# RWKV stage of a transformer block: TensorE keeps the emitted order, PSUM banks per stream, final norms as a stream in the next unit

## The chip, the cores and the metric

One core of a Trainium2 chip runs the whole program. TensorE (PE in the profile) multiplies, VectorE (DVE), ScalarE (ACT) and GpSimd (POOL) work on tiles in SBUF and read matmul results out of PSUM, and SyncE (SP) issues most of the DMAs. Each engine takes its own instructions in a fixed order; an instruction that waits for another engine holds up everything behind it on its own. The metric is the device time of one execution in microseconds, the median of the runs.

## The reference, cut to what matters

One layer: a modulated norm, one input projection, three groups of sequence mixers that all read that projection, an output projection, a mixture of experts and a final norm. The stage that the change touches is the RWKV-7 mixer, 12 heads of 64 channels over 256 context and 512 latent tokens, once forward and once backward:

```python
def _rwkv_scan(inp, s0):
    """RWKV-7: S = S diag(w) + (S (-kk)) (kk*a)^T + v k^T ; y = S r."""
    r, decay, k, v, kk, a = (jnp.moveaxis(t, 1, 0) for t in inp)
    def step(s, t):
        rt, wt, kt, vt, kkt, at = t
        sa = jnp.einsum('bhvk,bhk->bhv', s, -kkt)
        s = (s * wt[:, :, None, :] + sa[..., None] * (kkt * at)[:, :, None, :]
             + vt[..., None] * kt[:, :, None, :])
        return s, jnp.einsum('bhvk,bhk->bhv', s, rt)
    s_fin, ys = lax.scan(step, s0, (r, decay, k, v, kk, a))
    return jnp.moveaxis(ys, 0, 1), s_fin
...
    # _rwkv_mixer, after both directions are summed
    return (_head_norm(yl, g_norm, RWKV_GN_EPS, True) + bl) * jax.nn.sigmoid(gl)
```

## The kernel before, in words

The scan is computed in blocks of 64 tokens. Within a block the step-by-step recurrence becomes small matrices, among them the inverse of a lower triangular 64x64 matrix per head, direction and block. The work is cut into 18 **units** (3 groups of four heads, 6 token blocks each), numbered 0 to 17 here. A unit passes through three stages, each a Python generator, in three consecutive steps of `rwkv_all`:

- `rw_s1`, preparation: **c**, running sums of the decays by four matmuls per half (L702); the exponentials on ScalarE; the scaled keys **BK** and queries **AR** on VectorE and GpSimd (L712 to L716); **A**, products of the two, 32 matmuls for direction 0 and then 32 for direction 1 (L729); VectorE masks them out of PSUM into **AMa** and **AMr** (L734). Then SP issues eight DMAs that write the 16x16 diagonal blocks of AMa to DRAM (**s_ad**, L741) and one that reads them back in another layout (**Lay**, L742). **T** are transposes of BK (L750). I write A\* for the last A group of a unit.
- `rw_s2`, the inverse: on VectorE a **chain** of 15 rounds (product L776 into ptm, sum L778 into Tm) inverts the 16x16 blocks from Lay; two DMAs (**s_td**) write the result, sixteen (**ed**, L789) read it back in the layout that TensorE wants. Then four groups of inverse matmuls (L806), **I1** to **I4**, each of two halves of 16 instructions 64x64: I1 multiplies ed by Bo, ScalarE copies the result out (iY, L810); I2 to I4 are added up by VectorE (iF, Ef, L812). **V** is one more group (L770). At I1 the unit must have its ed.
- `rw_s3`, the scan over the unit's two blocks (x, y, s, k in tiles "ch" and "acc"; chX, chW, chS, rv on the other engines; L833 to L865). After the last token block of a head group the final norms `rwkv_fin` (L920 to L938: center, fin_sq, norm_bcast) run inside the same generator.

So in step k the preparation of unit k, the inverse of unit k-1 and the scan of unit k-2 are interleaved, together with **fill**: blocks of the input projection of later columns, six matmuls 128x512 each (two rows of weights by three products of the split fp32 numbers, L329), 240 blocks in all, which have nothing to do with the scan and need only weights. `weave` takes the next piece of whichever generator is furthest behind its share; `NKE` sets how many fill blocks the first and last steps get, NS2 and the other weights in the list the shares. What `weave` emits is a program order. The tile scheduler then orders the instructions of each engine anew, by when it believes their inputs to be ready, and all but the first matmul of a fill block are marked high priority, so that a block stays together (`first` and `high_priority` at L327).

PSUM tiles come in named rings: "g" has three banks (c, A, T, V, I and the norms share it), "ch" two, "acc" one, and fill has its own. Each half of an I group is a "g" tile of its own.

Of the kernel before, what the change touches and what calls it, by code (L numbers as in the profile page):

```python
# [19 lines left out]
P = 128  # L20
# [3 lines left out]
LC = 256  # L24
# [11 lines left out]
NS2 = 45  # L36
# [6 lines left out]
NKE = (12, 12, 12, 12)  # L43
# [8 lines left out]
class Kern:  # L52
    def __init__(self, tc, I, out):
        self.tc, self.nc, self.I, self.out = tc, tc.nc, I, out
        self.dram = {}
        self.gt1 = None

# [20 lines left out]
    def load_consts(self, cp, ps):  # L78
# [42 lines left out]
        with self.tc.tile_pool(name="prow", bufs=1) as pr:  # L121
            done = 0
            rest = list(order)
            while done < tot:
# [12 lines left out]
                nc.tensor.transpose(p[:, :used], vr[:used], self.ident[:used, :used])  # L137
# [7 lines left out]
    def norm_bcast(self, pool, ps, tag, sq, nt, scale, eps, op, bufs=2):  # L145
# [5 lines left out]
        for t in range(nt):  # L151
            nc.tensor.matmul(pn[:, t], sq[:, t * P:(t + 1) * P], self.ind2, start=True, stop=True)
# [10 lines left out]
        for t0 in range(0, nt, 4):  # L163
            n = min(4, nt - t0)
            p = ps.tile([P, 512], F32, name=tag, bufs=bufs)
            for t in range(n):
                nc.tensor.transpose(p[:, t * P:(t + 1) * P], rx[:, t0 + t], self.ident)
# [3 lines left out]
    def phase_h(self, ps, early):  # L171
# [13 lines left out]
        with tc.tile_pool(name="wa", bufs=5) as wa, tc.tile_pool(name="xp", bufs=1) as xp:  # L185
            for t in range(6):
# [10 lines left out]
                for k0 in range(0, KT, 4):  # L197
                    p = ps.tile([P, 4, P], F32, name=("pl", "pc")[k0 // 4 % 2], bufs=self.pb)
                    for k in range(4):
                        nc.tensor.transpose(p[:, k], xt[:, (k0 + k) * P:(k0 + k + 1) * P], self.ident)  # L200
# [4 lines left out]
            for j in range(4):  # L205
                pa = ps.tile([P, 256], F32, name="px", bufs=2)
                for k0 in range(0, KT, 2):
# [3 lines left out]
                    for k in range(2):  # L211
                        for s in range(2):
                            for hf in range(2):
                                b = 32 * (2 * s + hf)
                                nc.tensor.matmul(pa[b:b + 32, :], self.sil[:, k0 + k, :], w[:, s, k, hf * 256:(hf + 1) * 256],
# [7 lines left out]
                for q in range(2):  # L223
                    nc.tensor.transpose(pt[:, q], ar[:, q * P:(q + 1) * P], self.ident)
# [36 lines left out]
    def ada2_sum(self, blk):  # L261
        nc = self.nc
        for q in range(4):
            p = self.ps.tile([P, 512], F32, name="px", bufs=2)
            nc.tensor.matmul(p[:1], self.ones[:, :1], self.acc2[:, q], start=True, stop=True)
# [44 lines left out]
    def w_tile(self, col, n, lat, ctx, fill=None):  # L310
# [4 lines left out]
        for q in range(4):  # L315
# [113 lines left out]
    def rw_k(self, pr):  # L429
# [25 lines left out]
        for d in range(2):  # L455
            yield
            a = sp.tile([P, T], F32, name="o_a")
            for (s0, n) in ((0, LC), (LC, S)):
                p = ps.tile([P, 512], F32, name="px", bufs=2)
                nc.tensor.matmul(p[:, :n], wz[:96, 1, d], self.wa1[:96, 2 + d, s0:s0 + n], start=True, stop=True)  # L460
# [11 lines left out]
            for t0 in (0, 4):  # L472
                n = min(4, 6 - t0)
                p = ps.tile([P, 4, P], F32, name="px", bufs=2)
                for t in range(n):
                    nc.tensor.matmul(p[:, t], self.wa1[:97, d, (t0 + t) * P:(t0 + t + 1) * P], wz[:, 0, d], start=True, stop=True)
# [20 lines left out]
    def to_tokens(self, x, o):  # L497
# [3 lines left out]
        for t0 in range(0, nt, 4):  # L501
            n = min(4, nt - t0)
            p = self.ps.tile([P, 4, P], F32, name=tag, bufs=bufs)
            for t in range(n):
                nc.tensor.transpose(p[:, t], x[:, (t0 + t) * P:(t0 + t + 1) * P], self.ident)
            nc.vector.tensor_copy(o[:, t0:t0 + n], p[:, :n])

    def rw_r(self, pr):
# [9 lines left out]
        nc.tensor.matmul(p, self.blk, m, start=True, stop=True)  # L518
# [145 lines left out]
    def rw_s1(self, st, u, q, g):  # L664
# [33 lines left out]
        for i in range(2):  # L698
            pb = ps.tile([P, 2, 2, 2, 64], F32, name="g", bufs=3)
            for d in range(2):  # L700
                for j, x in enumerate((sgh, sgl)):
                    nc.tensor.matmul(pb[:, d], x[:, i, d], self.tri, start=(j == 0), stop=(j == 1))  # L702
# [20 lines left out]
        for d in range(2):  # L723
            pA = [ps.tile([P, 4, n, 64], F32, name="g", bufs=3) for _ in range(2)]
            for c in range(4):
                for h in range(2):
                    hs = slice(64 * h, 64 * h + 64)
                    for a in range(2):
                        nc.tensor.matmul(pA[h][64 * a:64 * a + 64, c].rearrange("p a t -> p (a t)"), BK[hs, 4 * d + c, a],  # L729
                                         AR[hs, 4 * d + c, :n].rearrange("p a t -> p (a t)"), start=True, stop=True)  # L730
# [15 lines left out]
        pT = [ps.tile([P, 8, 64], F32, name="g", bufs=3) for _ in range(2)]  # L746
        for c in range(8):
            for h in range(2):
                hs = slice(64 * h, 64 * h + 64)
                nc.tensor.transpose(pT[h][:, c], BK[hs, c].rearrange("p a t -> p (a t)"), self.ident[hs, hs])  # L750
# [6 lines left out]
    def rw_s2(self, st, u):  # L757
# [8 lines left out]
        p = ps.tile([P, 8, 64], F32, name="g", bufs=3)  # L766
        for c in range(8):
            for h in range(2):
                hs, ks = slice(64 * h, 64 * h + 64), slice(64 - 64 * h, 128 - 64 * h)
                nc.tensor.matmul(p[hs, c], AMa[ks, h, c], RV[ks, h, c], start=True, stop=True)  # L770
# [28 lines left out]
        for (o, lhs, rhs) in ((Y, Bo, Dd), (F1, Y, E), (F2, Y, F1), (Ef, Y, F2)):  # L799
            for c0 in (0, 4):  # L800
# [1282 lines left out]
```

## Time and profile before

| what | value |
|---|---|
| median of 3 runs | 3124.62 us (3121.7 to 3134.05) |
| the profiled execution, its own time | 3124.07 us |
| its span in the trace | 3122.3 us |
| TensorE busy | 2810.3 us, 90% of the span |
| VectorE, ScalarE, GpSimd busy | 1633.1, 859.9, 812.2 us |
| RWKV stage in the trace | about 789 to 1551 us |

The time outside the span is 1.8 us. A busy TensorE is not one at its peak: matmuls overlap, and PEclk shows which part of the full clock it was granted. Where a line says `[0.79 <-DMA ed<-s_td]`, the engine sat idle for 0.79 us before that row, and a DMA ended the wait.

### The profile page before, as it was taken

The page shows a single profiled execution, that of the slowest core. Times are in us where ns is not written, and L with a number is a line of the kernel's source. Part 1 is how long each engine was busy: PE and PEld are TensorE (multiplying, and loading weights), DVE is VectorE, ACT ScalarE, POOL GpSimd, SP SyncE. Part 2 cuts the span into 40 slices and gives each one's busy share as a digit, 9 for nine tenths or more (in the row PEclk, how much of TensorE's full clock was granted, in tenths as well). Part 3 has the DMA queues.
Part 4 walks back from the last instruction along what each step waited for, and adds up shares of the span by engine and source line. Part 5 has one row for each costly group of instructions (what it writes and reads, how often), then busy time and mean ns, then how long its engine had stood idle before and what let it go on. Part 6 is the DMA issues. An engine that isn't in the chain of part 4 may idle for free. (4 is left out here: it accounts for less than half of the span.)

```text
span 3122.3 us, 50607 instructions
## 1 busy us (share of the span) xinstructions
PE 2810.3 (90%) x19241; PEld 1825.2 (58%) x19241; DVE 1633.1 (52%) x3215; ACT 859.9 (28%) x1570; POOL 812.2 (26%) x765
## 2 busy tenths in 40 slices
PE   5989998988989989889789888799999999999997
PEld 3478777777677766667556666644344343434432
DVE  4275657685675554455375656624343342434335
ACT  4142332346432233222132332412122120212202
POOL 2232222221433432433343443411011010101101
PEclk9999999989999999999989899899999999999999
DMA  8767878887543443443383323499999999999996
GB/s 305 272 191 217 248 221 265 246 258 210 136 110 97 104 108 98 105 107 82 103 266 98 116 70 100 154 365 369 409 342 385 362 343 410 342 409 342 382 369 247
DMA packets 526878, 730.79 MB, mean 234 GB/s; under 512 B 121042, under 2 KB 343808, under 8 KB 525220
## 3 DMA queue, kind: packets, MB, share of 16 engines
q1 hardware_dynamic: 362832, 640.77, 57.9%
q10 hardware_dynamic: 161927, 81.17, 10.2%
q0 software_dynamic: 1872, 5.57, 0.6%
q8 instruction: 154, 2.52, 0.3%
q14 instruction: 93, 0.75, 0.1%
HBM read 672.50 MB, written 54.93 MB: 233 GB/s over the span
## 5 line engine op out<-in xcount | busy, mean ns | idle before, releaser
L1716 PE MATMUL pgu<-ring,xg 128*64 128x512 f32 x2048 | 487.1, 599 | 0.0
L307 POOL TENSOR_TENSOR wl<-wr,wh 128x512 fp32r<-128x512 f32 x191 | 263.8, 1382 | 666.9 <-ACT wh L306 606.9
L329 PE MATMUL pl<-hil,wh 128*128 128x512 f32 x928 | 404.2, 436 | 4.6 <-ACT hil L241 3.7
L329 PE MATMUL pl<-lol,wh 128*128 128x512 f32 x928 | 375.9, 405 | 0.2
L329 PE MATMUL pl<-hil,wl 128*128 128x512 f32 x928 | 371.5, 400 | 1.1 <-POOL wl L307 1.1
L306 ACT CAST wh<-wr 128x512 fp32r<-128x512 f32 x292 | 179.6, 619 | 532.2 <-PE pl L329 290.6
L1682 POOL TENSOR_TENSOR hl<-h,hh 128x512 fp32r<-128x512 f32 x64 | 99.4, 1554 | 861.7 <-ACT hh L1681 861.7
L1716 PEld LDWEIGHTS pgu<-ring,xg 128*64 128x64 f32 x2048 | 137.3, 136 | 254.1 <-issue 236.0
L1740 PE MATMUL py<-ring,hT 128*64 128x512 f32 x1024 | 257.0, 598 | 0.0
L259 DVE SCALAR_TENSOR_TENSOR acc<-w,sil,acc 128x512 f32<-128x512 f32 x240 | 201.4, 868 | 55.6 <-DMA w<-in_w_ada_dram 54.0
L329 PEld LDWEIGHTS pl<-hil,wh 128*128 128x128 f32 x928 | 178.9, 193 | 60.5 <-issue 15.1
L329 PEld LDWEIGHTS pl<-hil,wl 128*128 128x128 f32 x928 | 178.7, 193 | 42.2 <-POOL wl L307 1.8
L329 PEld LDWEIGHTS pl<-lol,wh 128*128 128x128 f32 x928 | 179.7, 194 | 38.1 <-issue 6.4
L1681 ACT CAST hh<-h 128x512 fp32r<-128x512 f32 x128 | 134.4, 1092 | 120.1 <-PE pc__20645 L1685 2.7
L1740 PEld LDWEIGHTS py<-ring,hT 128*64 128x64 f32 x1024 | 85.8, 136 | 129.7 <-issue 125.1
L329 PE MATMUL pc<-hic,wl 128*128 128x256 f32 x496 | 146.0, 295 | 12.9 <-DVE wl L307 8.7
L329 PE MATMUL pc<-hic,wh 128*128 128x256 f32 x496 | 145.8, 295 | 5.9 <-ACT hic L241 3.2
L329 PE MATMUL pc<-loc,wh 128*128 128x256 f32 x496 | 144.9, 293 | 1.2 <-DVE loc L242 1.2
L1748 DVE SCALAR_TENSOR_TENSOR yt<-py,Wsl,g 128x512 f32<-128x512 f32 x64 | 48.1, 751 | 161.1 <-PE py L1740 158.4
L1749 ACT CAST yeh<-yt 128x512 fp32r<-128x512 f32 x64 | 39.6, 619 | 290.0 <-DVE yt L1748 290.0
L1410 POOL TENSOR_TENSOR wol<-wo,woh 128x512 fp32r<-128x512 f32 x56 | 76.0, 1361 | 160.3 <-PE acc L1413 100.6
L776 DVE TENSOR_TENSOR ptm<-Tm,Lay 64x1 f32<-64x1 f32 (+2 forms) x270 | 106.9, 396 | 16.9 <-DMA Lay<-s_ad 10.2
(2216 smaller groups left out, 5074.9 us busy)
## 6 DMA issues: line engine op xcount, KB each, us to landing
ring<-in_moe_w_gate_dram SPq DMA_DIRECT2D x256, 512.0 KB
ring<-in_moe_w_up_dram SPq DMA_DIRECT2D x256, 512.0 KB
ring<-in_moe_w_down_dram SPq DMA_DIRECT2D x128, 1024.0 KB
wr<-in_w_in_dram ACTq DMA_DIRECT2D x288, 256.0 KB
w<-in_w_ada_dram SPq DMA_DIRECT2D x256, 256.0 KB
w<-in_w_ada_dram SPq DMA_DIRECT2D x64, 512.0 KB
wo<-in_w_out_dram SPq DMA_DIRECT2D x56, 256.0 KB
rv_xk<-d_xk SPq DMA_DIRECT2D x36, 256.0 KB
```

The source lines that it names most:

```text
L259: nc.vector.scalar_tensor_tensor(acc, w, self.sil[:, k, 0:1], acc, op0=OP.mult, op1=OP.add)
L306: nc.scalar.copy(wh[:, :, :n], wr[:, :, :n])
L307: (nc.vector if q in self.wdve else nc.gpsimd).tensor_tensor(wl[:, :, :n], wr[:, :, :n], wh[:, :, :n].bitcast(F32), op=OP.subtract)
L329: nc.tensor.matmul(o[:n], a[:, k, :n], r, start=(q == k == i == 0), stop=(q == k == 3 and i == 2))
L776: nc.vector.tensor_tensor(pt_[:, :t, :t], Tm[:, :t, :t], Lay[:, :t, t].rearrange("q (o s) -> q o s", o=1).to_broadcast([64, t, t]), op=OP. ...
L1410: nc.gpsimd.tensor_tensor(wl, w, wh.bitcast(F32), op=OP.subtract)
L1681: nc.scalar.copy(hh, h)
L1682: (nc.gpsimd if k else nc.vector).tensor_tensor(hl, h, hh.bitcast(F32), op=OP.subtract)
L1716: nc.tensor.matmul(p[64 * c:64 * c + 64], x[:, k, 64 * (e % 4):64 * (e % 4) + 64], g[:, :, k % 2, 256 * c:256 * c + 256], start=(k == 0), ...
L1740: nc.tensor.matmul(py[64 * c:64 * c + 64], ht[2 * pr + c][:, f % 2, 64 * (f // 2):64 * (f // 2) + 64], wgt[2 * pr + c, (col[0] // 1024, f ...
L1748: nc.vector.scalar_tensor_tensor(yt, py, W, self.g2[:, col[0]:sum(col)], op0=OP.mult, op1=OP.mult)
L1749: nc.scalar.copy(yh, yt)
```

## The change

Five things, all of them in or around the RWKV stage:

1. All matmuls and transposes go through `mm` and `tr`. While `self.pin` is set, which is during `rwkv_all` alone, the scheduler has to keep each of them in the order in which it was emitted. The high priority of the fill matmuls goes.
2. PSUM: "g" has two banks, for c, A and T; a new ring "g2" of one bank serves V and the I groups, both halves of a group in one tile; the final norms take banks of "ch".
3. `rw_s1` yields twice more after each direction's A (22 pieces, with the weight left at 18), the I groups yield at other places (48 pieces, NS2 45 to 48).
4. The final norms of a head group run as a stream of their own, with the weight NF = 40, one step later, so there are 21 steps instead of 20.
5. NKE goes from (12, 12, 12, 12) to (12, 12, 10, 10, 8).

```diff
-NKE = (12, 12, 12, 12)
+NKE = (12, 12, 10, 10, 8)
+NF = 40
...
+    def mm(self, *a, **k):
+        i = self.nc.tensor.matmul(*a, **k)
+        if self.pin:
+            self.tc.keep_in_program_order(i)
...
-                            first = k % self.wk == 0 and i == 0 or self.wk == 1
-                            with nullcontext() if first else self.tc.high_priority():
-                                nc.tensor.matmul(o[:n], a[:, k, :n], r, start=(q == k == i == 0), stop=(q == k == 3 and i == 2))
+                            self.mm(o[:n], a[:, k, :n], r, start=(q == k == i == 0), stop=(q == k == 3 and i == 2))
...
-            pA = [ps.tile([P, 4, n, 64], F32, name="g", bufs=3) for _ in range(2)]
+            pA = [ps.tile([P, 4, n, 64], F32, name="g", bufs=2) for _ in range(2)]
...
                     nc.vector.tensor_tensor(o[:, h, 4 * d:4 * d + 4], pA[h][:, :, a], self.msk[:, a:a + 1].to_broadcast([P, 4, 64]), op=OP.mult)
+            yield
+            yield
...
-        p = ps.tile([P, 8, 64], F32, name="g", bufs=3)
+        p = ps.tile([P, 8, 64], F32, name="g2", bufs=1)
...
-                p = ps.tile([P, 4, 64], F32, name="g", bufs=3)
-                for c in range(4):
+                for c in range(c0, c0 + 4):
                     for h in range(2):
                         hs = slice(64 * h, 64 * h + 64)
-                        nc.tensor.matmul(p[hs, c], lhs[hs, c0 + c], rhs[hs, c0 + c], start=True, stop=True)
-                    if c % 2:
-                        yield
+                        self.mm(p[hs, c], lhs[hs, c], rhs[hs, c], start=True, stop=True)
                 if o is Y:
-                    nc.scalar.copy(Y[:, sl], p)
+                    nc.scalar.copy(Y[:, sl], p[:, sl])
                 else:
-                    nc.vector.tensor_tensor(o[:, sl], p, E[:, sl], op=OP.add)
+                    nc.vector.tensor_tensor(o[:, sl], p[:, sl], E[:, sl], op=OP.add)
+                yield
...
-        for k in range(n + 2):
+
+        def fins(q):
+            for i in range(2):
+                yield from self.rwkv_fin(2 * q + i, self.rwy[:, i])
+
+        for k in range(n + 3):
...
-            if k >= 2:
-                gs.append((self.rw_s3(st[k - 2], *units[k - 2]), 7 if units[k - 2][1] < 5 else 47, *W3))
+            if 2 <= k < n + 2:
+                gs.append((self.rw_s3(st[k - 2], *units[k - 2]), 7, *W3))
+            if k >= 3 and units[k - 3][1] == 5:
+                gs.append((fins(units[k - 3][0]), NF))
...
+            self.pin = True
             drain([(self.rwkv_all(fill, NA * 16 // WK - RF), 1)])
+            self.pin = False
```

Ahead of the stage TensorE's order is the same in both kernels, and in the stages behind it nearly so. Within the stage three places are shown, the first where A\* of one unit meets I1 of the unit before it. TensorE before, from the last A of unit 8 on (the last row but one is the first of I1 of unit 7):

```order
L729 MATMUL g<-AR,BK 64x128 x4
L853 MATMUL ch<-rv,BKt 64x64 x8
L750 MATMUL g<-ident,BK 128x64 x2
L329 MATMUL pl<-hil,wh 128x512
L329 MATMUL pl<-lol,wh 128x512
L329 MATMUL pl<-hil,wl 128x512
L329 MATMUL pl<-hil,wh 128x512
L329 MATMUL pl<-lol,wh 128x512
L329 MATMUL pl<-hil,wl 128x512
L750 MATMUL g<-ident,BK 128x64 x3
L806 MATMUL g<-ed_6994,Bo 64x64
L750 MATMUL g<-ident,BK 128x64 x6
```

TensorE after, the same two groups (the two `g_11008` rows are I1 of unit 7, the last row is A\* of unit 8; nb_x and rv_y are final norms):

```order
L61 MATMUL g<-AR,BK 64x128 x4
L61 MATMUL g_11008<-ed_6994,Bo 64x64 x8
L66 MATMUL ch<-ident,nb_x 128x128 x2
L61 MATMUL ch<-rv_y,k_blk 128x256
L61 MATMUL g_11008<-ed_6994,Bo 64x64 x8
L61 MATMUL pl<-hil,wh 128x512
L61 MATMUL pl<-lol,wh 128x512
L61 MATMUL pl<-hil,wl 128x512
L61 MATMUL pl<-hil,wh 128x512
L61 MATMUL pl<-lol,wh 128x512
L61 MATMUL pl<-hil,wl 128x512
L61 MATMUL g<-AR,BK 64x128 x4
```

I1 of a unit has moved from one fill block behind A\* of the next unit to one fill block ahead of it; between A\* and I1 of the same unit there stand 11 blocks now, 13 before. This holds in nearly every unit from 5 on; in the first units it was up to 19 blocks before and is 11 now. The waits at I1 in the changed kernel, in program order (each name is a semaphore that the instruction waits for):

```order
L61 MATMUL g_11008<-ed_6994,Bo 64x64 [waits DMAHW5_49,DMAHW7_49,DMAHW3_49,DMAHW1_49]
L61 MATMUL g_11008<-ed_6994,Bo 64x64 [waits DMAHW4_49,DMAHW6_49,DMAHW2_49,DMAHW0_49]
L61 MATMUL g_11008<-ed_6994,Bo 64x64 x6
L66 MATMUL ch<-ident,nb_x 128x128 [waits DVE_49,PE_49]
L66 MATMUL ch<-ident,nb_x 128x128
L61 MATMUL ch<-rv_y,k_blk 128x256 [waits DVE_49]
L61 MATMUL g_11008<-ed_6994,Bo 64x64 [waits Activation_49]
L61 MATMUL g_11008<-ed_6994,Bo 64x64 x7
```

The first two wait for the ed DMAs, and the second half of the group for ScalarE, which copies the first half out of the same bank; before, a half went to a bank of its own. The second place is VectorE in the chain of unit 8, from its third round on. Before:

```order
L776 TENSOR_TENSOR ptm<-Tm,Lay 64x3x3
L307 TENSOR_TENSOR wl<-wr,wh 128x512
L812 TENSOR_TENSOR iF_11124<-g,ed_6993 128x256 x2
L778 TENSOR_REDUCE Tm<-ptm 64x3
L776 TENSOR_TENSOR ptm<-Tm,Lay 64x4x4
```

After:

```order
L788 TENSOR_TENSOR ptm<-Tm,Lay 64x3x3
L790 TENSOR_REDUCE Tm<-ptm 64x3
L788 TENSOR_TENSOR ptm<-Tm,Lay 64x4x4
L790 TENSOR_REDUCE Tm<-ptm 64x4
L788 TENSOR_TENSOR ptm<-Tm,Lay 64x5x5
```

The weight split wl and the additions iF have left the chain; a second BK and two AR of the next unit, which stood between the last rounds, stand behind the chain now. In units 1 and 3 the changed order has eight additions of the convolution (o_a, L550) inside the chain instead of one and none. The third place is the start of the stage on TensorE. Before, the last of six fill blocks ahead of the first c:

```order
L329 MATMUL pl<-hil,wh 128x512
L329 MATMUL pl<-lol,wh 128x512
L329 MATMUL pl<-hil,wl 128x512
L702 MATMUL g<-tri,rv_sgh 128x256
L702 MATMUL g<-tri,rv_sgl 128x256
```

After, from the last transpose of the stage ahead:

```order
L66 MATMUL px<-ident,o_a 128x128 x2
L61 MATMUL pl<-hil,wh 128x512
L61 MATMUL pl<-lol,wh 128x512
L61 MATMUL pl<-hil,wl 128x512
L61 MATMUL pl<-hil,wh 128x512
L61 MATMUL pl<-lol,wh 128x512
L61 MATMUL pl<-hil,wl 128x512
L61 MATMUL g<-tri,rv_sgh 128x256
L61 MATMUL g<-tri,rv_sgl 128x256
```

One block stands ahead of the first c instead of six, and eight instead of two between it and A\* of unit 0. At the end of the stage I1 of unit 17 comes 10 blocks behind its A\* instead of 13, and 22 blocks instead of 21 follow it.

## Rows read from the trace of the kernel before

**Rows 1.** Windows: two stretches of the stage; PE, PEld, DVE, ACT, POOL busy, PEclk, DMA share, GB/s.
```profile
789.00:982.00 193.00, 175.76 (x2032) 135.45 (x2031) 135.38 (x325) 68.31 (x132) 79.39 (x87) 0.94 0.45 114
982.00:1470.00 488.00, 444.23 (x5524) 336.02 (x5525) 258.88 (x704) 133.95 (x289) 192.63 (x218) 0.95 0.40 100
```

**Rows 2.** What TensorE waited for in the stage: line, releaser, us in total, times, longest.
```profile
PE g L167 <- DVE nb_x L159: 15.8, 9, 3.3
...
PE g L806 <- DMA ed<-s_td: 4.5, 3, 3.0
```

**Rows 3.** Timeline of TensorE: A\* of units 0, 5, 8 and 17, and the stage's last transposes.
```profile
798.88 1.01 PE L729 MATMUL g<-AR,BK 64*64 64x64 f32 x20
...
981.00 0.45 PE L729 MATMUL g<-AR,BK 64*64 64x128 f32 x8
...
1106.02 0.45 PE L729 MATMUL g<-AR,BK 64*64 64x128 f32 x8
...
1469.62 0.45 PE L729 MATMUL g<-AR,BK 64*64 64x128 f32 x8
...
1550.27 0.66 PE L167 MATMUL g<-ident,nb_x 128*128 128x128 f32 x2 [3.29 <-DVE nb_x L159]
```

**Rows 4.** Windows: a steady stretch in the middle of the stage.
```profile
1122.00:1160.00 38.00, 34.73 (x434) 25.81 (x435) 22.96 (x62) 12.79 (x24) 15.38 (x17) 1.00 0.43 109
```

**Rows 5.** Timeline of SP's queue for unit 8, from s_ad to ed.
```profile
1107.75 4.90 SPq L741 DMA_DIRECT2D s_ad<-AMa  x8
...
1134.96 9.00 SPq L789 DMA_DIRECT2D ed<-s_td  x16
```

**Rows 6.** Timeline of TensorE: the first half of I1 of unit 8.
```profile
1145.28 0.65 PE L806 MATMUL g<-ed,Bo 64*64 64x64 f32 x8 [0.79 <-DMA ed<-s_td]
```

**Rows 7.** Timeline of TensorE: a fill block and an I group; then ScalarE's copies, by tile.
```profile
1115.67 0.50 PE L329 MATMUL pl<-hil,wh 128*128 128x512 f32 x1
...
1117.25 1.15 PE L806 MATMUL g<-iF,iY 64*64 64x64 f32 x32
1118.33 0.50 PE L329 MATMUL pl<-hil,wh 128*128 128x512 f32 x1
...
L810 ACT COPY iY<-g x36: 354/373/384, 840.5 to 1506.8; 128x256 f32<-128x256 f32 x36
```

**Rows 8.** Timeline of VectorE in the chain of unit 8: other work inside it.
```profile
1118.78 0.69 DVE L307 TENSOR_TENSOR wl<-wr,wh 128x512 fp32r<-128x512 f32 x1
1119.38 0.75 DVE L812 TENSOR_TENSOR iF<-g,ed 128x256 f32<-128x256 f32 x2
...
1130.68 0.96 DVE L715 TENSOR_TENSOR AR<-rv_r,ex 128x256 f32<-128x256 f32 x1
1131.56 0.37 DVE L778 TENSOR_REDUCE Tm<-ptm 64x15 f32<-64x225 f32 x1
```

**Rows 9.** Timeline: ed of unit 0; A\* and ed of unit 10; I1 of unit 17.
```profile
827.13 8.59 SPq L789 DMA_DIRECT2D ed<-s_td  x16
...
1181.11 0.45 PE L729 MATMUL g<-AR,BK 64*64 64x128 f32 x8
...
1214.24 8.53 SPq L789 DMA_DIRECT2D ed<-s_td  x16
...
1503.86 0.33 PE L806 MATMUL g<-ed,Bo 64*64 64x64 f32 x2
```

**Rows 10.** Tile o_a in the first stretch: ns min/median/max of one, first and last start.
```profile
L550 DVE SCALAR_TENSOR_TENSOR o_a<-pl,par,o_a x48: 656/678/746, 800.5 to 917.0; 128x441 f32<-128x441 f32 x24, 128x448 f32<-128x448 f32 x12, 128x504 f32<-128x504 f32 x12
```

**Rows 11.** The stage's start: the tile rv_sgl that the first c needs; then TensorE.
```profile
L680 DVE TENSOR_TENSOR rv_sgl<-rv_sg,rv_sgh x3: 675/692/1673, 788.4 to 828.8; 128x512 fp32r<-128x512 f32 x3
...
789.27 0.28 PE L702 MATMUL g<-tri,rv_sgh 128*128 128x256 f32 x1
...
793.34 0.79 PE L729 MATMUL g<-AR,BK 64*64 64x64 f32 x32 [1.56 <-POOL AR L713]
795.60 0.56 PE L729 MATMUL g<-AR,BK 64*64 64x64 f32 x12 [1.47 <-POOL AR L713]
```

More of the change, by code (lines that the diff above doesn't have):

```diff
@@ L1 @@
 import math
-from contextlib import ExitStack, nullcontext
+from contextlib import ExitStack
 from functools import partial
@@ L35 @@
 OAN, OBN = 30, 32
-NS2 = 45
+NS2 = 48
 NR = 4
@@ L264, in ada2_sum @@
             p = self.ps.tile([P, 512], F32, name="px", bufs=2)
-            nc.tensor.matmul(p[:1], self.ones[:, :1], self.acc2[:, q], start=True, stop=True)
+            self.mm(p[:1], self.ones[:, :1], self.acc2[:, q], start=True, stop=True)
             nc.scalar.copy(self.acc2[:1, q], p[:1])
@@ L517, in rw_r @@
         p = ps.tile([P, S], F32, name="px", bufs=2)
-        nc.tensor.matmul(p, self.blk, m, start=True, stop=True)
+        self.mm(p, self.blk, m, start=True, stop=True)
         nc.vector.tensor_tensor(m, self.vt[:, 0, LC:], p, op=OP.mult)
@@ L745, in rw_s1 @@
             nc.gpsimd.tensor_tensor(Bo[hs], AMa[hs, h], self.ndg[hs, None, :].to_broadcast([64, 8, 64]), op=OP.mult)
-        pT = [ps.tile([P, 8, 64], F32, name="g", bufs=3) for _ in range(2)]
+        pT = [ps.tile([P, 8, 64], F32, name="g", bufs=2) for _ in range(2)]
         for c in range(8):
@@ L832, in rw_s3 @@
                     for hs in H:
-                        nc.tensor.matmul(pX[hs, e], AR[hs, 2 * e + c, 0], St[hs, e], start=True, stop=True)
+                        self.mm(pX[hs, e], AR[hs, 2 * e + c, 0], St[hs, e], start=True, stop=True)
                 if g > 1:
@@ L864, in rw_s3 @@
                     for h in range(2):
-                        nc.tensor.matmul(pYo[H[h], 2 * e + c], RV[:, h, 2 * e + c], AMr[:, h, 2 * e + c], start=False, stop=(c == 1 and e == 3))
+                        self.mm(pYo[H[h], 2 * e + c], RV[:, h, 2 * e + c], AMr[:, h, 2 * e + c], start=False, stop=(c == 1 and e == 3))
             yield
@@ L880, in rw_s3 @@
                     nc.vector.tensor_tensor(b[:, ::-1], b[:, ::-1], o[:, 1], op=OP.add)
-            if g == 5:
-                for i in range(2):
-                    yield from self.rwkv_fin(2 * q + i, self.rwy[:, i])
         yield
@@ L932, in rwkv_fin @@
                 yield
-            nb = yield from self.norm_bcast(mp, ps, "g", sq, 2, 1.0 / 64, 64e-5, OP.add, bufs=3)
+            nb = yield from self.norm_bcast(mp, ps, self.ft[0], sq, 2, 1.0 / 64, 64e-5, OP.add, bufs=self.ft[1])
             for (p, _, n) in nb:
@@ L1034, in ml_gates @@
         for j in range(6):
-            nc.tensor.matmul(p[:, j], selp[:, j], dm[:, 1], start=True, stop=True)
+            self.mm(p[:, j], selp[:, j], dm[:, 1], start=True, stop=True)
         nc.vector.tensor_copy(self.mdec, p)
@@ L1412, in out_cols @@
                     for t in range(4):
-                        nc.tensor.matmul(po[t], a[:, i, t * P:(t + 1) * P], b, start=(i == j == 0), stop=(i == n - 1 and j == 2))
+                        self.mm(po[t], a[:, i, t * P:(t + 1) * P], b, start=(i == j == 0), stop=(i == n - 1 and j == 2))
                 yield
@@ L1454, in out_last @@
                     for j, (a, b) in enumerate(((yh, wh), (yl, wh), (yh, wl))):
-                        nc.tensor.matmul(p, a[:, i, t * P:(t + 1) * P], b[:, i, cs], start=(i == j == 0), stop=(i == n - 1 and j == 2))
+                        self.mm(p, a[:, i, t * P:(t + 1) * P], b[:, i, cs], start=(i == j == 0), stop=(i == n - 1 and j == 2))
                 nc.vector.tensor_tensor(self.x1[:, t, cs], self.x1[:, t, cs], p, op=OP.add)
@@ L1479, in route_setup @@
         p = self.ps.tile([P, 36], F32, name="lt", bufs=1)
-        nc.tensor.matmul(p, self.ones, sr, start=True, stop=True)
+        self.mm(p, self.ones, sr, start=True, stop=True)
         nc.vector.tensor_tensor(self.cb, self.cb, p, op=OP.add)
@@ L1576, in route_slots @@
         for t in range(4):
-            nc.tensor.matmul(pc, ltb[:, 1], Ab[:, t], start=(t == 0), stop=(t == 3))
+            self.mm(pc, ltb[:, 1], Ab[:, t], start=(t == 0), stop=(t == 3))
         self.over = rp.tile([P, 32, 7], F32, name="over")
@@ L1915, in run @@
             mid, rw, ml, gl, oc = (ExitStack() for _ in range(5))
-            self.ps = pool(mid, "ps2", space=PSUM)
+            self.ps = pool(rw, "ps2", space=PSUM)
+            self.ft = ("ch", 2)
             self.rp = pool(rw, "rp")
@@ L1934, in run @@
             fill = self.pipe(jobs[:NA])
+            self.pin = True
             drain([(self.rwkv_all(fill, NA * 16 // WK - RF), 1)])
+            self.pin = False
             drain([(fill, 1)])
             rw.close()
+            self.ps = pool(mid, "ps2b", space=PSUM)
+            self.ft = ("g", 3)
             right.close()
```

85 lines of the change are left out of this document (46 added, 39 removed).

## The prediction

> **What bounds the kernel now.** I read the windows of the stage first. TensorE is busy 175.8 of 193 us up to 982 us and 444.2 of 488 us behind it, at 0.94 and 0.95 of the full clock; VectorE is at 70% and then 53% [rows 1]. So TensorE is near the limit there, with some 9% to win. Then its waits: the largest groups are the transposes of the final norms (15.8 us, 9 times) and many small ones; waits at I1 for the ed DMAs are only 4.5 us [rows 2]. Removing waits can therefore bring some tens of us at best.
>
> Second, how long a unit takes. A\* of unit 0 ends at 798.88 + 1.01 = 799.9, of unit 5 at 981.45, of unit 17 at 1470.1, and the last transposes end at 1550.9 [rows 3]. That gives 181.6 us for five early units (36.3 each), 488.6 for twelve later ones (40.7 each), and 80.9 for the tail. In a stretch at full clock TensorE's own work fills 34.7 of 38 us, and 38 is about a unit, so its floor is near 34.7 per unit [rows 4].
>
> Third, the path that is not on TensorE. Behind A\* of unit 8 (ends 1106.47) come the masks, eight s_ad DMAs from 1107.75, Lay, the chain on VectorE, s_td, and sixteen ed DMAs, issued from 1134.96 to 1143.96 [rows 5]; I1 starts at 1145.28, released by the last of them after 0.79 us of waiting [rows 6]. **A\* to I1 is 38.8 us**, as long as a whole unit, and an ed is ready 1.3 us after its issue ends. With that 1.3, unit 0 has 827.13 + 8.59 + 1.3 - 799.9 = 37.1, unit 10 has 1214.24 + 8.53 + 1.3 - 1181.56 = 42.5, and unit 17, whose I1 starts at 1503.86, has 33.8 [rows 3, 9]. Before, this is hidden: I1 stands one block behind A\* of the next unit, so the path may take a unit's period and 2 us more.
>
> **The change part by part.** *The kept order.* I1 of unit u now stands one block ahead of A\* of unit u+1, and nothing may overtake a waiting I1. So A\* of the next unit cannot start until ed has landed, and its own path starts from there: a closed loop, and its period is the path plus what stands on TensorE from I1 to A\*. An I group of 16 instructions takes 1.08 us (32 records, 1117.25 to 1118.33), so half of it 0.54; a fill block 1117.25 - 1115.67 = 1.58 [rows 7]; the last A group 0.45 [rows 3]. Queued behind I1 are all fill blocks and the scan, none of which can fill the wait, whatever is ready.
>
> *One bank per I group.* The order with its waits shows the second half waiting for the copy of the first. The copy takes 0.373 us [rows 7]; with 0.1 us each for the hand-over I take 0.6. Bounds: 0 if the hand-over hides in the pipeline, 1.0 if ScalarE is busy with an exponential. Four times per unit that is 2.4 us on TensorE, and 0.6 in the loop. So I1 to A\* is 0.54 + 0.6 + 0.54 + 1.58 + 0.45 = **3.7 us**. Before, the two halves ran with no wait between them. The Trainium skill, "PSUM — Partial Sum Buffer", section "PSUM bank collisions raise a hardware error", says that two engines may not touch one bank in the same partitions at a time, even at other addresses, and so asks for a guard by bank; it speaks against this edit, since a copy out of half a bank then holds the matmuls into the other half. No row of before shows such a pair. Were there no such wait, the loop would be 0.6 x 17 = 10 us shorter in all.
>
> *A shorter chain.* In unit 8 the changed order takes out wl (0.60 us up to the next row), the iF pair (0.75) and the AR ahead of the last sum (0.88), and one more BK and AR of about 0.35 each, 2.9 in all [rows 8]. Other units keep one of these, so I take 2.6; bounds 1 and 4. Steady period: 38.8 - 2.6 + 3.7 = 39.9, twelve times 479, against 488.6: **-10 us**. In this the waits at the final norms are included; TensorE's floor, 34.7 + 2.4 = 37.1, lies below.
>
> *The early units.* They now have 11 blocks between A\* and I1, not up to 19, so the loop binds them too. Unit 0: 37.1 + 3.7 = 40.8. Units 1 and 3 have eight convolution steps of 0.678 us in the chain [rows 10], 5.4 more: 45.3 each. Units 2 and 4: 39.9 each. Sum 211.2 against 181.6: **+30 us**. Here is the largest term: the early units had the shortest period because nothing tied I1 to the next A\*.
>
> *The start.* The first c starts at 789.27, right behind rv_sgl (from 788.4, 0.7 long) [rows 11], so its input sets it and it cannot come earlier. TensorE gets there five blocks sooner and waits about 8 us. From c to A\* of unit 0 it took 10.6 us, with two blocks and two waits of 1.56 and 1.47; now eight blocks stand there. 10.6 - 3.0 + 6 x 1.58 = 17.1, less about 2 because blocks ran slower than 1.58 behind those waits: 15, so **+5** (bounds +3 and +8).
>
> *The tail.* Ed of unit 17 is due 33.8 us behind A\*, but ten blocks and small groups reach I1 in some 27, so TensorE waits 7. From I1 to the end it took 1550.9 - 1503.9 = 47.1 us [rows 3, 9]; now one block more (1.6) and four half waits (2.4). **+4** (bounds 0 and +12, the latter if the norms, a step later, lose their cover).
>
> *At nothing:* two "g" banks instead of three. A of direction 1 needs the masks of direction 0 gone; the two new yields put fill between, and without that cover the cost is up to 1 us per unit, 18 in all. The norms in "ch" may hold up the scan, which nothing in the loop waits for. NKE moves blocks between steps and removes none.
>
> **Sum:** +5 + 30 - 10 + 4 = +29 on the profiled execution's 3124.1 (1.8 of it outside the span), which is 0.5 below the median: **3153 us**.
>
> **The rivals.** About 0.5% (15.6 us) is what a measurement of this kernel can tell from no change.
>
> *The loop at its shortest: no change.* If all steady units have the path of unit 17, 33.8, the period is 37.5 and twelve of them 450, -39; with +5, +30 and +4 the time stays at **3124**. For it: a stalled TensorE sends less work to VectorE and SP, and the queues run freer. Against it: unit 17 has no unit behind it whose preparation competes, and units 8 and 10 need 38.8 and 42.5. It holds for steady periods between 36.1 and 38.8.
>
> *TensorE stays the bound: faster.* If the path falls under 37.1 - 3.7 = 33.4 us in all units, the early ones too, ed is ready when I1 comes, and a unit costs 37.1: 17 x 37.1 = 631 against 670.2, -39 + 5 + 4, **3094 us**. Measurably faster begins at a mean period of 38.0. For it: TensorE's waits at the norms and the scan have their fill ahead of them, and the shortest path seen still has iF in its chain. Against it: none of the four paths read is below 33.4.
>
> *SP and the norms lengthen the path: slower still.* The changed SP order puts rv_xk, which waits for both BK, ahead of ed in most units; a wait there delays all sixteen. With unit 10 as the pattern, 42.5 - 2.6 + 3.7 = 43.6 per steady unit, +35: **3198 us**. A clock that falls after each wait at I1 would act the same way, since the 3.7 us behind it would then run slower.
>
> **How the numbers follow.** My forecast, a loop of about 40 us, 0.45 (3136 to 3178 by its own bounds: 1 to 4 us off the chain, half waits 0 to 1); no change 0.20; faster 0.21; slower still 0.14. The range takes in the faster rival's centre and the slower one's: 3092 to 3200, with about a tenth left out on each side. Over 0.5% faster: 0.23, the faster rival and a little of the next; within 0.5%: 0.22; over 0.5% slower: 0.55.
>
> **What the profile after would show.** If right: I1 waits for DMA ed in nearly every unit, 3 to 6 us each and 50 to 90 us in all, where 4.5 stand now; A\* to A\* of about 40 us both early and late; TensorE's busy share of the stage near 86%; a wait of 6 to 9 us at the first c; waits of the second halves for ScalarE and VectorE of some 0.6 us; hardly a wait at the norms' transposes. The fill blocks then make no wait shorter, since they stand behind it. It would be wrong if A\* to I1 falls to 33 us because the chain or SP's queue is faster than in the rows read, or if the early units keep 36 us; both show in the distance from A\* to I1 alone.

## The result, and the profile after

The changed kernel took 3213.8 us in the median (3210.2 to 3218.6), the kernel before 3127.8 on the same chips: the ratio is 1.0276, with a 95% interval of 1.0248 to 1.0304. The forecast was slower by 0.9%; it is slower by 2.8%, beyond the range. The profiled execution has a span of 3208.4 us against 3122.3.

Nearly all of it lies in the RWKV stage. The stage behind it starts at 1653.4 us instead of 1564.2, 89 us later; 2 to 3 of these are there already when the stage begins, and 3 come back further on. The windows answer to [rows 1]; the columns are the same, and the last row is the tail:

```profile
788.00:1037.00 249.00, 196.62 (x2104) 144.24 (x2105) 134.86 (x328) 72.79 (x139) 78.16 (x88) 0.87 0.37 94
1037.00:1556.00 519.00, 444.53 (x5522) 330.98 (x5519) 256.96 (x706) 134.71 (x289) 190.77 (x217) 0.94 0.37 93
1556.00:1636.00 80.00, 70.67 (x793) 55.01 (x791) 30.20 (x84) 17.33 (x34) 24.10 (x24) 0.96 0.24 60
```

TensorE is busy 79% of the first stretch, where it was 91%, and 86% of the second, where it was 91%; in the first it had 0.87 of its clock, where it was 0.94. What it waited for in the stage, as in [rows 2]:

```profile
PE g L61 <- DMA ed<-s_td: 30.0, 9, 9.1
PE g L61 <- DVE iF L822: 21.8, 30, 1.1
PE g L61 <- ACT iY L820: 21.7, 20, 4.4
PE g L61 <- DVE Ef L822: 10.8, 15, 1.7
...
PE g L61 <- ACT rv_sgh L689: 7.2, 1, 7.2
...
PE ch L66 <- DVE nb_x L171: 1.1, 4, 0.5
```

The waits at the final norms are gone (15.8 to 1.1). In their place stand 54 us of waits at the I groups for ScalarE's copies and VectorE's additions (65 waits; 56 of them, 46 us, are at the second half of a group, which waits for the bank), and 30 us at I1 for ed. All idle time of TensorE in the stage, the wait at the first c included, is 141 us; before it was 69.

Now the units, as in [rows 3]: the last A groups of units 0, 5 and 17, and the stage's last transposes.

```profile
809.60 0.34 PE L61 MATMUL g<-AR,BK 64*64 64x64 f32 x8
...
1035.86 0.71 PE L61 MATMUL g<-AR,BK 64*64 64x128 f32 x8
...
1555.16 0.45 PE L61 MATMUL g<-AR,BK 64*64 64x128 f32 x8
...
1641.10 0.44 PE L66 MATMUL ch<-ident,nb_x 128*128 128x128 f32 x2 [0.18 <-DVE nb_x L171]
```

From end to end that is 226.6 us for the five early units (45.3 each, before 36.3), 519.0 for the twelve later ones (43.3 each, before 40.7) and 85.9 for the tail (before 80.9). A\* of unit 0 ends 10 us later. So +10, +45, +30 and +5: 90.

What one turn looks like is seen from I1 of unit 3 to A\* of unit 4, in TensorE's timeline, which answers to [rows 6, 7]:

```profile
981.72 1.55 PE L61 MATMUL g<-ed,Bo 64*64 64x64 f32 x16 [6.19 <-DMA ed<-s_td]
983.73 1.12 PE L61 MATMUL g<-ed,Bo 64*64 64x64 f32 x16 [0.46 <-ACT iY L820]
984.78 0.79 PE L61 MATMUL pl<-hil,wh 128*128 128x512 f32 x1
985.37 0.63 PE L61 MATMUL pl<-lol,wh 128*128 128x512 f32 x1
985.80 0.63 PE L61 MATMUL pl<-hil,wl 128*128 128x512 f32 x1
...
987.64 0.70 PE L61 MATMUL g<-AR,BK 64*64 64x128 f32 x8
```

TensorE waited 6.19 us for the ed DMAs, did the first half, waited for ScalarE's copy, did the second half, one fill block and A\*. The matmuls of the block stand 0.43 us apart where they stand 0.23 apart at full clock. The window shows the clock; the line under it is the window of I1 of unit 11, in front of which TensorE did not wait:

```profile
981.00:989.00 8.00, 6.79 (x62) 5.32 (x62) 0.62 (x2) 1.85 (x4) 0.99 (x1) 0.50 0.02 4
1330.20:1334.00 3.80, 3.25 (x59) 2.37 (x52) 0.43 (x1) 0.74 (x2) 0.00 (x0) 1.00 0.94 254
```

The granted clock was 0.50, the lower of its two levels (1.2 of 2.4 GHz), right behind the idle time. I1 to A\* took 988.34 - 981.72 = 6.6 us here, not 3.7. In unit 11, at granted clock 1.00, it took 1333.91 - 1330.26 = 3.65:

```profile
1330.26 0.65 PE L61 MATMUL g<-ed,Bo 64*64 64x64 f32 x16
1331.37 0.68 PE L61 MATMUL g<-ed,Bo 64*64 64x64 f32 x16 [0.46 <-ACT iY L820]
...
1333.57 0.34 PE L61 MATMUL g<-AR,BK 64*64 64x64 f32 x8
```

The Trainium skill, "PSUM — Partial Sum Buffer", section "PSUM bank collisions raise a hardware error", asks that two engines be kept apart by bank; the wait for the copy at the second half, 0.46 us in these rows, is that guard at work, and the trace agrees with it.

### The profile page after: what moved, and what is told of

It is laid out like the page before. It is cut to its first block, busy times and chain, and to the rows that moved or that the text cites. A ratio compares the mean times of both kernels' runs of the same rounds, so it can differ in the third digit from the quotient of the medians.

```text
span 3208.4 us, 50560 instructions
## 1 busy us (share of the span) xinstructions
PE 2830.8 (88%) x19241; PEld 1828.4 (57%) x19241; DVE 1625.9 (51%) x3215; ACT 863.7 (27%) x1574; POOL 808.0 (25%) x765
## 5 line engine op out<-in xcount | busy, mean ns | idle before, releaser
L61 PE MATMUL pl<-hil,wh 128*128 128x512 f32 x928 | 411.1, 444 | 4.6 <-ACT hil L253 3.7
L319 DVE TENSOR_TENSOR wl<-wr,wh 128x512 fp32r<-128x512 f32 x101 | 72.4, 718 | 90.8 <-ACT wh L318 76.2
```

The lines of the kernel that those rows point to most:

```text
L61: i = self.nc.tensor.matmul(*a, **k)
L319: (nc.vector if q in self.wdve else nc.gpsimd).tensor_tensor(wl[:, :, :n], wr[:, :, :n], wh[:, :, :n].bitcast(F32), op=OP.subtract)
```

## The experiments

Each kernel ran beside the kernel before on one chip, and the ratios are to that. "Free order" means that the scheduler may move TensorE's instructions, as before.

**1. The changed kernel in free order.** The pin is off and the fill's high priority is back:

```diff
-            self.pin = True
             drain([(self.rwkv_all(fill, NA * 16 // WK - RF), 1)])
```

> The changed kernel without the kept order: the scheduler may move TensorE's instructions again and the later matmuls of a fill block have high priority as before; banks, yields, the norms' own stream and NKE stay as changed. Closed-loop theory (the time went because I1 stands ahead of the next A*, so a period is the path A* to I1 plus the stretch I1 to A*): in this order I1 stands on either side of A*, within 2 blocks, and the path has 10 to 12 blocks and more in the early units, so most of the loss returns, 3130 to 3150 us. Bank theory (the time went at the second halves of the I groups, V and A, which wait for evictions wherever they stand): the waits remain, since the banks are the same, 3165 to 3190 us.

Measured: 3135.3 us, ratio 1.0040 (1.0023 to 1.0056). Of the 2.8% the kept order makes 2.4, some 74 us; banks, yields, norms and NKE together cost about 12. The one-bank groups wait here too, but less (21.5 us instead of 54): the bank theory's 3165 is ruled out as a cost by itself. The scheduler's own order holds the pattern too: in 8 of the 12 later units it put I1 ahead of the next A\*, by one block at most.

**2. The kept order alone,** in the kernel before: `mm` and `tr` with the pin around `rwkv_all`, the high priority gone, nothing else.

> The kernel before with the kept order alone: old banks (both halves of an I group in banks of their own), old yields, norms and NKE. In its order I1 stands one block behind A* of the next unit, so there is no closed loop. Closed-loop theory: little is lost, 3125 to 3145 us, of which some 10 at the start, where the first c is held ahead of five fill blocks. Bank theory: the same, 3125 to 3145. If the kept order itself costs, through every wait that fill may no longer pass: over 3170 us.

Measured: 3172.8 us, 1.0164 (1.0126 to 1.0202). Neither theory allowed that; it is the third case, that the kept order itself costs. In this order I1 stands behind A\* of the next unit. What TensorE waited for is other things that stand directly behind their cause:

```profile
PE g L65 <- DVE AMr L744: 20.5, 11, 4.8
PE g L60 <- DMA ed<-s_td: 13.8, 3, 5.7
PE ch L60 <- DVE rv L856: 13.6, 9, 2.9
```

The transposes T come right behind A\* and need the banks that the masks (AMr) still read; before, fill was moved in between. So this kept order costs where nothing was placed between a producer and its reader, without a loop. Its later units took 43.4 us from A\* to A\*, as long as those of the changed kernel, its early ones 40.7: by itself the length of a later unit does not tell the loop from other waits in a kept order.

**3. A\* earlier.** The changed kernel, with the preparation's share of a step cut so that I1 stands one block behind the next A\*:

```diff
-W1, W2, W3 = (0, .9), (0, 1), (0, 1)
+W1, W2, W3 = (0, .7), (0, 1), (0, 1)
```

> The changed kernel with the preparation given a share of 0.7 of the step instead of 0.9: A* stands two to three blocks earlier and I1 one block behind A* of the next unit, as before the change; everything else as changed. Closed-loop theory: the waits for ed nearly vanish, the five early units fall from 45 to 38 us and the later ones from 43 to 38 or 39, 3125 to 3150 us. Bank theory: only the 34 us of waits at I1 and some clock come back, 3165 to 3185 us.

Measured: 3175.9 us, 1.0168 (1.0135 to 1.0202). The early units fell from 45.3 to 39.8, near the closed-loop theory's 38; the later ones only from 43.3 to 42.0, and the total is the bank theory's. The wait for ed fell from 30.0 to 8.6 us, that at the I groups' second halves grew:

```profile
PE g L61 <- ACT iY L820: 28.3, 16, 5.9
PE g L61 <- DVE iF L822: 27.4, 33, 2.1
PE g L61 <- DVE Ef L822: 15.3, 18, 1.8
PE g L61 <- DMA ed<-s_td: 8.6, 2, 7.5
```

The same edit had put T next to I1, and the order of the other engines with it; it opened one thing and tightened another, so it doesn't decide.

**4. A shorter chain.** Seven of the fifteen rounds:

```diff
-        for t in range(1, 16):
+        for t in range(1, 8):
```

> The changed kernel with 7 of the 15 rounds of the chain on VectorE; the last eight are left out, so the 16x16 inverses are incomplete. The chain is some 7 us shorter, TensorE's order stays. Closed-loop theory: A* to I1 falls from 38 to about 32 us and the period with it until TensorE's own work bounds it at 37 to 38: 17 periods by 5 to 6 us, about 3120 us. Bank theory: TensorE is the bound already, only the waits for ed go, 3170 to 3185 us.

Measured: 3189.4 us, 1.0206 (1.0177 to 1.0234). The expectation's "TensorE's order stays" was not so. Each round is also a piece in the interleaving, and without eight of them I1 moved up to 9 blocks behind its A\* and 3 ahead of the next one. The path fell to 28 us as meant, and the stretch from I1 to A\* grew to 15: the loop stayed shut, and the run decided nothing until it was repeated (run 9).

**5. The banks of before under the kept order:** one ring "g" of three for c, A, T, V and I, each half of an I group a tile of its own.

```diff
-            p = ps.tile([P, 8, 64], F32, name="g2", bufs=1)
             for c0 in (0, 4):
+                p = ps.tile([P, 4, 64], F32, name="g", bufs=3)
```

> The changed kernel with the banks of before for c, A, T, V and I (one ring of three, each half of an I group a tile of its own); kept order, yields, norms and NKE as changed, so TensorE's order is that of the changed kernel. Kept-order theory (what stands late in the order is waited for, and each wait is followed by a stretch at half clock): the 58 us of waits inside the I groups fall under 15, but T and c now wait for banks that the masks hold, 15 to 25 as in the run with the old kernel's order kept; 3170 to 3190 us. Closed-loop theory: I1 still stands ahead of A*, only 0.6 us per period go, 3200 to 3210 us.

Measured: 3203.2 us, 1.0244 (1.0222 to 1.0267). The waits for VectorE's additions fell, and the time went straight to the wait for ed:

```profile
PE g L61 <- DMA ed<-s_td: 51.7, 16, 12.9
PE g L61 <- ACT iY L820: 13.4, 16, 3.3
...
PE g L61 <- DVE Ef L822: 8.6, 16, 0.6
```

TensorE reached I1 sooner and waited there, 16 times instead of 9. This is the closed-loop theory's number. The wait at the second half of I1 itself stayed (12 waits, 11.6 us; 13 and 14.1 in the changed kernel), so this run does not test the 0.6 us that it adds to the period.

**6. The halves apart.** The same two extra yields, put between the halves of a group:

```diff
                     nc.vector.tensor_tensor(o[:, sl], p[:, sl], E[:, sl], op=OP.add)
                 yield
-            yield
-            yield
+                yield
```

> The changed kernel with the two extra yields of an I group moved between its halves: a fill block stands now between the halves of a group, and next to nothing between one group and the next, which share the bank too. Kept-order theory: the waits inside the groups go, a part returns at the first half of the next group; 58 us become 25 to 35, with the clock 3180 to 3195 us. Closed-loop theory: I1 to A* does not get shorter, 3205 to 3220 us.

Measured: 3206.5 us, 1.0246 (1.0213 to 1.0278), again the closed loop's number: the waits for ed rose to 36.4 us in 14 units.

**7. Three repairs at once:** runs 3 and 6 together, and five fill blocks ahead of `rwkv_all`.

> The changed kernel with its order still kept, but A* earlier (share 0.7), the halves apart, and five fill blocks ahead of the first c. If the waits of the kept order are what costs and add up: 38 for A* (measured), 20 to 30 for the halves, 8 to 10 for the start, 3133 to 3150 us. If they stand in for each other (a wait removed here comes back at the next late row): 3160 to 3175 us.

Measured: 3159.0 us, 1.0115 (1.0093 to 1.0136), 1 us below the lower edge of "they stand in for each other". The wait of 7 us at the first c is gone, and a unit from 5 on takes 40.4 us, as before the change. The early units stay at 41.9.

**8. The norms' own stream alone,** with the new NKE, in the kernel before, free order and old banks.

> The kernel before with the norms' own stream and the new NKE alone: free order, old banks, old yields. If the 15.8 us of waits at the norms' transposes go and nothing takes their place: 3105 to 3115 us, faster than both kernels. If the scheduler fills them otherwise or the last step grows: 3118 to 3130 us.

Measured: 3113.5 us, 0.9971 (0.9954 to 0.9988). This part of the change is a gain, about 0.3%, and the only version of the study that computes everything and is faster than both kernels.

**9. The short chain in TensorE's unchanged order.** As run 4, with eight empty pieces in place of the rounds left out; row for row the changed kernel's order on TensorE.

```diff
+        for _ in range(8):
+            yield
         Dm = mp.tile([64, 16, 16], F32, name="Dm", tag="ptm")
```

> As the run with the short chain (7 of 15 rounds, the inverses incomplete), but the eight pieces that the left-out rounds gave to the interleaving are kept empty, so that TensorE's order is row for row that of the changed kernel; in the run before this one I1 had moved two blocks up, to 9 behind its A*. Closed loop alone: the path falls from 37 to 28 us with I1 still 11 blocks behind A*, the period to TensorE's floor, 3115 to 3135 us. Two bounds that stand side by side (the loop, and TensorE's own work with the waits inside the I groups and the clock behind them, 41 to 42 us per unit): the waits for ed go and the others stay, 3170 to 3195 us.

Measured: 3119.8 us, 0.9985 (0.9971 to 0.9999). With ed ready 27 us behind A\* instead of 37, 2.9% come back, some 91 us (the medians, from two chips, differ by 94): all that the change had cost, and a little more. The waits inside the I groups are still there (49 us), so they are no second bound of 41 us per unit. A\* of units 5 and 17:

```profile
998.08 0.45 PE L61 MATMUL g<-AR,BK 64*64 64x128 f32 x8
...
1472.09 0.45 PE L61 MATMUL g<-AR,BK 64*64 64x128 f32 x8
```

That is 474.0 us for twelve units, 39.5 each. TensorE waited for ed only in unit 0, so this is its own pace in this order, with the waits inside the I groups.

**10. The short chain and the halves apart.**

> The short chain with the pieces kept (7 of 15 rounds, the inverses incomplete), and the halves of the I groups apart as in the run before. Two bounds: apart alone gave 7 us because the loop held; with the loop open the waits inside the groups count, so both together give more than the sum of the two, 3135 to 3160 us. If they add up: the short chain's time less 7.

Measured: 3101.9 us, 0.9937 (0.9913 to 0.9960). Apart is worth 18 us once the loop is open, and was worth 7, within the noise, while it was shut. Both together came out 33 us below the range given for two bounds, because run 9 was already below its own.

**11. More fill in the early steps.** Run 7, with three more blocks in each of steps 1 to 5 and one less in the fifteen later ones.

> The kernel with three repairs (A* earlier, halves apart, five fill blocks ahead), with three more fill blocks in each of the steps 1 to 5 and one less in each of the later fifteen. If the early units wait for a path of 45 to 50 us that has convolution steps in its chain, as their waits for ed of 13 and 7 us suggest: the blocks fill waits there and shorten the later steps, 3135 to 3148 us. If the early units are TensorE-bound or the later ones need the blocks as cover: 3155 to 3170 us.

Measured: 3140.9 us, 1.0068 (1.0047 to 1.0088). The early units took as long (41.3) with three blocks more in each, and the later ones fell to 38.9. The early units were waiting, not working.

**12. The control: the short chain in free order.**

> The control for the short chain: the run with free order (banks, yields and norms as changed) with 7 of 15 rounds and the pieces kept, the inverses incomplete. If the gain of 94 us under the kept order came from the closed loop, there is little to win where the order is free: its waits for ed were 15.6 us, so 3110 to 3130 us against 3135. If it came from the 7 to 9 us per unit that VectorE no longer works, it comes here as well: 3045 to 3080 us.

Measured: 3081.1 us, 0.9872 (0.9855 to 0.9888): 54 us less than run 1, at the edge of the second case. So either the path limits the free order as well, or VectorE's work counts. Runs 13 and 14 part them for the kept order. For the free order the traces speak for the path: in run 1 TensorE waited for ed 13 times (15.4 us), in this run twice (1.8 us).

**13. The path back without the work.** Run 9, with four DMAs in a row from DRAM to DRAM between s_td and ed:

```diff
+        for nx in self.s_hop:
+            nc.sync.dma_start(nx[u], cur[u])
+            cur = nx
```

> The short chain with the pieces kept (7 of 15 rounds, the inverses incomplete; TensorE's order that of the changed kernel), and four DMAs in a row, DRAM to DRAM, between s_td and ed. The path A* to I1 gets some 9 us longer again and VectorE gets no work back. If the path is the cause of what the short chain won under the kept order: back to 3195 to 3225 us. If VectorE's work was: it stays at 3115 to 3130 us.

Measured: 3456.3 us, 1.1065 (1.1026 to 1.1104). The four hops lengthened the path by 24 us rather than 9, because SP has other DMAs between them in its order, some of which wait. The time followed: TensorE waited for ed in every unit.

```profile
PE g L61 <- DMA ed<-s_hop: 308.6, 18, 23.1
```

A\* of units 5 and 17 give the period:

```profile
1085.41 0.45 PE L61 MATMUL g<-AR,BK 64*64 64x128 f32 x8
...
1779.54 0.71 PE L61 MATMUL g<-AR,BK 64*64 64x128 f32 x8
```

(1780.25 - 1085.86) / 12 = 57.9 us. Over these twelve units the time from the end of A\* to the start of I1 is 51.6 us in the mean. The rest, 6.3 us, is I1 to the next A\*; behind the wait for ed the granted clock of this stretch was 0.50 to 0.62 in every unit:

```profile
1256.23 1.65 PE L61 MATMUL g<-ed,Bo 64*64 64x64 f32 x16 [18.48 <-DMA ed<-s_hop]
...
1260.33 0.79 PE L61 MATMUL pl<-hil,wh 128*128 128x512 f32 x1
1260.92 0.63 PE L61 MATMUL pl<-lol,wh 128*128 128x512 f32 x1
```

**14. The work back without the path.** Run 9, with rounds 8 to 15 executed behind the DMAs that write the result out:

```diff
         for i in range(EY):
+            t = 8 + i
+            if t < 16:
+                nc.vector.tensor_tensor(p2[:, :t, :t], Tm[:, :t, :t],
...
+                nc.vector.tensor_reduce(Tm[:, :t, t], p2[:, :t, :t], axis=mybir.AxisListType.X, op=OP.add)
             yield
```

> The short chain with the pieces kept, and the eight long rounds executed on VectorE behind the DMAs that write the result out, so that nothing waits for them but the queue: all of VectorE's work is there again, the path stays some 9 us shorter (the values are those of 7 rounds), TensorE's order is that of the changed kernel. If the path is the cause: 3115 to 3140 us. If VectorE's work is: 3195 to 3215 us.

Measured: 3144.7 us, 1.0069 (1.0046 to 1.0093), 5 us above the range given for the path. By the ratios VectorE's work costs 0.8%, some 26 of the 91 us, which leaves 65 to the path. A\* of units 5 and 17:

```profile
1007.88 0.45 PE L61 MATMUL g<-AR,BK 64*64 64x128 f32 x8
...
1499.10 0.45 PE L61 MATMUL g<-AR,BK 64*64 64x128 f32 x8
```

That is 40.9 us a unit, with all of VectorE's work and no wait for ed in any unit.

**15. Two queues for ed,** eight of the sixteen DMAs issued by ScalarE, in run 8's kernel.

> The run with the norms' own stream in free order, with eight of the sixteen ed DMAs issued by ScalarE instead of SP. If the path A* to I1 limits the free order too, as the control suggests: 4 us less path in a unit, 3090 to 3108 us against 3113.5. If ScalarE, which then stands at s_td in its own order, holds up its copies and casts: 3115 to 3140 us.

Measured: 3144.7 us, 1.0063 (1.0032 to 1.0095), 0.9% slower than run 8 and 5 us above the second case. The path from A\* to ed got 2 us shorter in the mean of units 5 to 16 (41.1 to 38.8), and T waited for the masks instead, 21 us where run 8 had under 2:

```profile
PE g L751 <- DVE AMr L735: 11.0, 5, 3.6
PE g L751 <- DVE AMa L735: 9.9, 5, 4.1
```

That fits a ScalarE held up by the waits it now issues behind, but where in its queue was not followed further.

## Why the prediction was right or wrong

**What held.** The mechanism: I1 ahead of the next A\*, in an order that nothing may pass, closes a loop, and a period is the path from A\* to I1 plus the stretch from I1 to A\*. Runs 9, 13 and 14 show it. TensorE's order is the same in all three and in the changed kernel; with ed ready 27 us behind A\* the period of a later unit is 39.5 and TensorE sets it, with the path at 51.6 it is 57.9, and VectorE's work without the path costs 26 of the 91 us again (40.9 a unit). Runs 5 and 6 show it from the other side: the waits inside the groups, in part removed, turn into waits for ed. The largest loss per unit in the early units held too, as did the tail (+5 against +4) and the norms' waits that vanish.

**The step that failed** is the sum "I1 to A\* is 0.54 + 0.6 + 0.54 + 1.58 + 0.45 = 3.7 us", priced from rows at full clock. Where the clock stayed at 1.00 and the wait at 0.46 us, the sum held: 3.7 us in units 2, 11 and 12. Where TensorE had waited for ed it ran this stretch, or most of it, at the lower level: 6.6 us in the rows of unit 3. The mean of I1 to A\* was 6.5 us in the early units and 4.9 in the later ones. That is 2.8 us too little five times and 1.2 twelve times, 28 of the 60 us that were missed. An estimate of the parts: without its idle time such a stretch takes some 3.2 us at full clock, and eight of them (units 0, 1, 3 to 6, 14 and 15), at a granted clock of 0.50 to 0.83, took 18 us more than that together; the idle time in the seventeen stretches is 6 us more than 0.6 each; what is left is mostly rows of other streams. So the clock is the larger part, not all. The longest stretch, 10.4 us in unit 4, followed no wait for ed: its second half waited for ScalarE's copy, which stood behind a cast that waited for a DMA (rv_sg), and the clock was low behind that wait.

```profile
1031.20 1.12 PE L61 MATMUL g<-ed,Bo 64*64 64x64 f32 x16 [4.39 <-ACT iY L820]
```

The prediction had the clock as a rival, "A clock that falls after each wait at I1 would act the same way", and gave it no number; in a loop it belongs in the sum, because the loop makes the waits behind which the clock was low in these rows.

**The second error** lies in "38.8 - 2.6", 36.2 us for the path of a later unit. A\* to I1 measured 38.4 in the mean of units 5 to 16. The ed were ready after 37.0, so the path itself was 0.8 off; SP and the norms did not lengthen it to the 39.9 of the slower rival. The other 1.4 is TensorE: in seven of the twelve units it reached I1 after ed was there and did not wait, in the others it waited, and a loop pays the later of the two every time. I had set the loop's 39.9 against TensorE's floor of 37.1 and taken the larger of two means, where the mean of the larger one counts; and the floor was low, since TensorE's own pace in this order is 40.9 with all of VectorE's work (run 14) and 39.5 without a part of it (run 9). Twelve times 2.2 is 26 us. For the early units the path was right, 38.5 forecast and 38.8 measured.

**The start** was +10, not +5. TensorE waited 7.24 us at the first c as forecast (about 8), but this c came at 791.50 us, 2.2 later than before, since its input did. From the middle of the wait on the clock was at the lower level for 10 us, which I had left out, and from c to A\* it took 18.5 us, not 15. So 28 + 26 + 5 + 1 make the 60. The forecast's own bounds, 3136 to 3178, were too narrow as well: 1 to 4 us off the chain in sixteen units and half waits of 0 to 1 give some 3118 to 3187.

**What the trace was to show.** "I1 waits for DMA ed in nearly every unit, 3 to 6 us each and 50 to 90 us in all" was wrong: nine units and 30 us. So was "A\* to A\* of about 40 us": 45.3 early and 43.3 late. The rest of the loop's price shows as other things, half-clock matmuls and waits for a copy behind I1. Busy share (84%), the waits of the second halves (0.8 us each, 0.6 forecast) and the norms came as described.

**The kept order** is a cost of its own beside the loop: run 2 loses 49 us without I1 ahead of A\*. I had costed it only through the loop, and by that sum run 2 would have come out at 3125 to 3145. Four kernels make a table of order and chain: the kept order costs 2.4% with the whole chain (the changed kernel against run 1) and 1.1% with the short one (run 9 against run 12). So some 38 of its 74 us hang on the long chain, by its path or its work, and some 35 are there without it.

**What stays open.** In free order the short chain won 54 us too (run 12). Its parts were not separated there: the path seems to limit the free order in most later units, as its 15 us of waits for ed say, but how much VectorE's work counts was not measured. What makes up the 35 us that the kept order costs with the short chain was not taken apart either. Nor were the 12 to 22 us taken apart by which banks and yields cost in free order (runs 1 and 8).

## What to carry to other kernels

When an order is pinned, look for pairs in which a late result stands ahead of the instruction that starts the next one's path; the period is then the path plus that stretch, and the stretch has to be priced at the clock that the wait leaves. Two streams that bound a period together cost the mean of the later one, so a repair of one of them can show little until the other is open: the halves apart won 7 us, within the noise, with the loop shut and 18 with it open. An experiment that drops work from an interleaved generator must keep its pieces, or it moves everything behind it.

## What the runs showed of the hardware

Idle time of TensorE brought time at the lower clock with it: the idle time in the stage grew from 69 to 141 us, and the time at the lower level (0.50) from 72 to 137 us; in run 13, where TensorE was idle for 376 us, it was 382. Four DMAs in a row from DRAM to DRAM, 128 KB each, added 24 us to the path, with SP's other DMAs between them.
